# A one-layer hybrid decoder on eight cores: channel-major inputs, three column blocks, and norm sums moved off TensorE

## The chip, the cores and the metric

The program runs on all 8 cores of one Trainium2 chip, each with one of the eight prompt sequences (2048 positions) and 16 of the 128 samples. Nothing is exchanged between cores; all read the same weights. The metric is the device time of the slowest core in microseconds. Most executions agree within 0.3%; some fall into a second, slower state in which one die's or both dies' granted TensorE clock is lower.

The engines are named as the profile names them: PE is TensorE, PEld its weight loads, DVE the vector engine, ACT the scalar engine, POOL is GpSimd, SP the sync engine that issues most small transfers.

## The reference, cut to what matters

```python
D_MODEL, BATCH, SEQ, DEC_BATCH, DEC_SEQ = 1024, 8, 2048, 128, 1
D_FF, P_DIM, CHUNK, CONV_W = 2816, 256, 128, 3

def layer(h, p, prev_a, prev_ffn, ...):
    xn = rmsnorm(h, g_mix)
    x_a, b_a, c_a, uv, ga, gb = split(xn @ w_in)          # 7168 columns
    a_conv, new_a = causal_dwconv(c_a * x_a, w_conv_a, prev_a)
    y_a = (b_a * a_conv) @ w_out_a
    u, v = split(gelu(uv)); v = rmsnorm(v, g_v)
    s = chunk_spatial(v, w_spatial, b_spatial)            # 128-position chunks
    y_b = (u * s) @ w_out_b
    h = h + (sigmoid(ga) * y_a + sigmoid(gb) * y_b) @ w_o
    up = rmsnorm(h, g_ffn) @ w_up                          # 5632 columns
    up_c, new_ffn = causal_dwconv(up, w_conv_ffn, prev_ffn)
    fa, fb = split(up_c)
    h = h + (gelu(fa) * fb) @ w_down
    gate = sigmoid(rmsnorm(h, g_ple) @ w_ple_gate)
    return h + gate * (p @ w_ple), new_a, v[last chunk], new_ffn
# the same layer for prompt and samples, then a final rmsnorm
```

## The kernel before

It keeps activations with channels on the partitions and positions along the row, and goes over the sequence in two passes of 1024 positions. Stages within a pass, by the letters that the code uses: AB (load, norm, v), C (short convolution), D (spatial gating), E (merge), F (output projection), G (up projection and its convolution), H (down projection), I (gate and final norm), O (y out). Weights stream through a ring of eight slots. Each block has 512 positions; the 16 samples are a third, 16-column block of pass 1.

Four parts matter. First, x arrives with positions on the partitions, and TensorE transposes it in and y out:

```python
for hf in range(2):                                   # x in, per 128 positions
    for kk in range(4):
        P.op("pe", lambda e, ...: e.transpose(out=pz[:, kk*128: kk*128+rows],
             in_=xt[0:rows, k*128:(k+1)*128], identity=idf[0:rows, 0:rows]), ...)
# ... and stage O, per 128 positions: 8 transposes of h, then a scaling, then the store
```

Second, a norm's sum of squares is eight matmuls with a matrix of ones per block, each fed by a square of ACT:

```python
class NormAcc:
    def add(self, k, b):
        while len(self.pend_mm) >= 2:
            self.pend_mm.pop(0)[1]()
        # ...
        def emit_sq():
            sq, sqr = sqR.get()
            P.op("act", ... activation(out=sq[:, 0:n], in_=h[:, k, c0:c0+n], func=AF.Square))
            self.pend_mm.append((bi, lambda: P.op("pe", lambda e: e.matmul(
                pst[:, 0:n], lhsT=ones[:], rhs=sq[:, 0:n], start=(cnt == 0), stop=(cnt == 7)), ...)))
```

Third, in stage G the up-projected rows are copied to SBUF with a two-column carry ahead of them, and the taps of the convolution read that copy:

```python
P.op("act", ... copy(out=ux[:, 2+q*512: 2+(q+1)*512], in_=pp[:, 0:512]))
P.op("act", ... activation(out=acc[:, q*512:(q+1)*512], in_=pp, func=AF.Identity, scale=wcf(2, cc)))
for tap in (0, 1):
    P.op("dve", ... scalar_tensor_tensor(out=acc[:, 0:1024], in0=ux[:, tap:tap+1024],
         scalar=wcf(tap, cc), in1=acc[:, 0:1024], op0=ALU.mult, op1=ALU.add))
# ... one channel pair later: gelu on ACT, product act = gelu(a) * b on POOL (1024 wide)
```

Fourth, a weight slab is a slice of the plain matrix, rows of 256 columns, and the first slab is asked for only when all of x has landed:

```python
src = w[:, c0:c0 + 256].rearrange("(k p) n -> p k n", p=128)
xtra = [("xst", 0), ("xst", 1), ("xst", 2), ("xst", 3), ("pst",)] if i == 0 else []
P.dma("pool", (lambda e, ...: e.dma_start(out=dst, in_=src)), f"wr{s}", reads=xtra, writes=res)
```

Of the kernel before, what the change touches and what calls it, by code (L numbers as in the profile page):

```python
# [19 lines left out]
TT = 1040  # L20

class Prog:
# [11 lines left out]
    def _deps(self, eng, reads, writes):  # L34
        deps = {}
        for r in reads:
            t = self.last_write.get(r)
            if t is not None and deps.get(t[0], 0) < t[1]:
                deps[t[0]] = t[1]
        for w in writes:  # L40
            t = self.last_write.get(w)
            if t is not None and deps.get(t[0], 0) < t[1]:
                deps[t[0]] = t[1]
            rd = self.readers.get(w)
            if rd:
                for k, v in rd.items():
                    if deps.get(k, 0) < v:
                        deps[k] = v
# [96 lines left out]

def bcast_mid(ap, reps):
    pairs = [list(x) for x in ap.ap]
    assert len(pairs) == 2, pairs
    return bass.AP(ap.tensor, ap.offset, [pairs[0], [0, reps], pairs[1]])

def build_program():
# [9 lines left out]
    x_d = din("x", [SEQ, D]); xs_d = din("xs", [NS, D])  # L161
    p_d = din("p", [SEQ, PD]); ps_d = din("ps", [NS, PD])
    sa_d = din("sa", [NS, 2, D]); sf_d = din("sf", [NS, 2, 2 * DFF])
    g_mix = din("g_mix", [D]); g_v = din("g_v", [D]); g_ffn = din("g_ffn", [D])
    g_ple = din("g_ple", [D]); g_final = din("g_final", [D])
    w_in = din("w_in", [D, NIN]); w_conv_a = din("w_conv_a", [3, D])
    w_out_a = din("w_out_a", [D, D]); w_out_b = din("w_out_b", [D, D]); w_o = din("w_o", [D, D])
    w_spatial = din("w_spatial", [8, 128, 128]); b_spatial = din("b_spatial", [8, 128])
    w_up = din("w_up", [D, 2 * DFF]); w_conv_ffn = din("w_conv_ffn", [3, 2 * DFF])
    w_down = din("w_down", [DFF, D]); w_ple_gate = din("w_ple_gate", [D, D]); w_ple = din("w_ple", [PD, D])  # L170
    ident_d = din("ident", [128, 128]); tril_d = din("tril", [128, 128])

    y_d = dout("y", [SEQ, D]); ys_d = dout("ys", [NS, D])
    ca_d = dout("ca", [2, D]); cas_d = dout("cas", [NS, 2, D])
    cv_d = dout("cv", [128, D]); cvs_d = dout("cvs", [NS, D])
    cf_d = dout("cf", [2, 2 * DFF]); cfs_d = dout("cfs", [NS, 2, 2 * DFF])

    es = contextlib.ExitStack()
    with es:
        def sb(name, shape, dt):  # L180
# [3 lines left out]
        xn = sb("xn", [128, 8, TT], BF16)  # L184
        R1 = sb("R1", [128, 9216 + 2 * 8 * TT], BF16)
        vn3 = R1[:, 0:9216].rearrange("p (t f) -> p t f", t=9)
        m3 = R1[:, 0:8 * TT].rearrange("p (k t) -> p k t", k=8)
        ab = R1[:, 9216:9216 + 8 * TT].rearrange("p (k t) -> p k t", k=8)
        us = R1[:, 9216 + 8 * TT:9216 + 16 * TT].rearrange("p (k t) -> p k t", k=8)
        act = R1[:, 0:22 * TT].rearrange("p (k t) -> p k t", k=22)  # L190
        R1f = R1[:, :].bitcast(F32)
        xst = R1f[:, 0:8192].rearrange("p (t f) -> p t f", t=8)
        pst_all = R1f[:, 8192:10240].rearrange("p (t f) -> p t f", t=8)
        xss = R1f[0:NS, 10240:11264]
        pss_all = R1f[0:NS, 11264:11520]
        pT = sb("pT", [128, 2, TT], BF16)
        ring = sb("ring", [128, 8, 2048], BF16)
        rs = sb("rs", [128, TT], F32)
        idf = sb("idf", [128, 128], F32); idb = sb("idb", [128, 128], BF16)
        tril = sb("tril", [128, 128], F32)  # L200
        ones = sb("ones", [128, 128], BF16)
        WsT = sb("WsT", [128, 8, 128], BF16)
        Ds = sb("Ds", [16, 8, 16], BF16)
        w00 = sb("w00", [16, 8], F32)
        bbcw = sb("bbcw", [128, 1032], F32)
        bbc = bbcw[:, 0:1024].rearrange("p (j t) -> p j t", j=8)
        gvbc = sb("gvbc", [128, 1024], F32)
        gfbc = sb("gfbc", [128, 1024], F32)
        rtok = sb("rtok", [128, 16], F32)
        cols1 = sb("cols1", [128, 64], F32)  # L210
        cols2 = sb("cols2", [128, 128], F32)
        wcfT = sb("wcfT", [128, 132], F32)
        carry_a = sb("carry_a", [128, 2, 8], F32)
        carry_f = sb("carry_f", [128, 2, 44], F32)
        saT = sb("saT", [128, NS, 2, 8], F32)
        sfT = sb("sfT", [128, NS, 2, 44], F32)
        oAs = sb("oAs", [128, NS, 2, 8], F32)
        oFs = sb("oFs", [128, NS, 2, 44], F32)
        ssv = sb("ssv", [128, 16], F32)
        rv = sb("rv", [128, 16], F32)  # L220
        big = [sb(f"big{i}", [128, 1024], F32) for i in range(4)]
        pbf = [sb(f"pbf{i}", [128, 256], BF16) for i in range(2)]
        sqall = sb("sqall", [128, 2064], BF16)
        sqb = [sqall[:, i * 512:(i + 1) * 512] for i in range(4)]
        sqwide = sqall[:, :].bitcast(F32)
        NTMP = 8
        tmpall = sb("tmpall", [128, NTMP * 516], F32)
        tmpf = [tmpall[:, i * 516:(i + 1) * 516] for i in range(NTMP)]
        widef = [tmpall[:, 2 * j * 516: 2 * j * 516 + 1032] for j in range(NTMP // 2)]
        ps = [es.enter_context(nc.psum_tensor(f"pq{i}", [128, 512], F32)) for i in range(8)]  # L230

        bigR = Rot([(big[i], ("big", i)) for i in range(4)])
        pinR = Rot([(None, pbf[i], ("pin", i), ("pbf", i)) for i in range(2)])
        sqR = Rot([(sqb[i], ("sq", i)) for i in range(4)])
        tmpR = Rot([(tmpf[i], [("tmp", i, "a"), ("tmp", i, "b")]) for i in range(NTMP)])
        wideR = Rot([(widef[j], [("tmp", 2 * j, "a"), ("tmp", 2 * j, "b"), ("tmp", 2 * j + 1, "a"), ("tmp", 2 * j + 1, "b")])
                     for j in range(NTMP // 2)] + [(bbcw, ["bbc"]), (sqwide, [("sq", i) for i in range(4)])])
        class PsRot:
            def __init__(self):
                self.i = 0  # L240
                self.reserved = set()

            def get(self):
                while True:
                    b = self.i % 8
                    self.i += 1
                    if b not in self.reserved:
                        return ps[b], ("ps", b)

            def reserve(self):  # L250
                t, r = self.get()
                self.reserved.add(r[1])
                return t, r

            def release(self, r):
                self.reserved.discard(r[1])

        psR = PsRot()
        scr = sb("scr", [128, 2], F32)
        epsT = sb("epsT", [128, 1], F32)  # L260

        def pstag(i):
            return ("ps", i)

        def gcol(gi, k):
            return cols1[:, gi * 8 + k: gi * 8 + k + 1]

        def wca(tap, j):
            return cols1[:, 32 + tap * 8 + j: 32 + tap * 8 + j + 1]

        def wcf(tap, c):
            r = tap * 44 + c
            if r < 128:
                return cols2[:, r:r + 1]
            return cols1[:, 56 + r - 128: 56 + r - 128 + 1]

        def stage_inputs(pss):
            r0 = pss * 1024
            P.dma("sp", (lambda e: e.dma_start(out=pst_all, in_=p_d[r0:r0 + 1024, :].rearrange("(t q) f -> q t f", q=128))),
                  "xp", reads=["R1busy"], writes=[("pst",)])  # L280
            for hf in range(4):
                P.dma("sp", (lambda e, hf=hf: e.dma_start(
                    out=xst[:, hf * 2:(hf + 1) * 2, :],
                    in_=x_d[r0 + hf * 256: r0 + (hf + 1) * 256, :].rearrange("(t q) f -> q t f", q=128))),
                    f"xs{hf}", reads=["R1busy"], writes=[("xst", hf)])
            if pss == 1:
                P.dma("sp", (lambda e: e.dma_start(out=xss, in_=xs_d[:, :])), "xq0", reads=["R1busy"], writes=[("xss",)])
                P.dma("sp", (lambda e: e.dma_start(out=pss_all, in_=ps_d[:, :])), "xq1", reads=["R1busy"], writes=[("pss",)])

        outs_tok = []  # L290
        stg0, stg0r = big[0], ("big", 0)
        stg1, stg1r = big[1], ("big", 1)
        setup = []

        def sdma(eng, out, in_, writes, **kw):
            setup.append((eng, out, in_, writes, kw))

        sdma("sp", idf[:], ident_d[:, :], ["idf"])
        sdma("sp", tril[:], tril_d[:, :], ["tril"])
        sdma("sp", bbcw[:, 0:1024], b_spatial.rearrange("j t -> (j t)").partition_broadcast(128), ["bbc"])  # L300
        sdma("sp", gvbc[:], g_v.partition_broadcast(128), ["gvbc"])
        sdma("sp", gfbc[:], g_final.partition_broadcast(128), ["gfbc"])
        sdma("sp", stg0[0:8, 0:128], g_mix.rearrange("(j p) -> j p", p=128), [stg0r])
        sdma("sp", stg0[8:16, 0:128], g_ffn.rearrange("(j p) -> j p", p=128), [stg0r])
# [85 lines left out]
        def slab_items():  # L390
            items = []

            def std(w, c0):
                items.append(("std", w, c0))
# [796 lines left out]
```

## Time and profile before

| | before |
|---|---|
| median of 6 runs | 1310.89 us (1308.83 to 1511.96; two slow) |
| spans of the cores in the profile | 1296.3 to 1311.1 us |
| mean granted clock of the cores | 0.963 to 0.968 |
| PE busy | 94% |

The chain and the windows are in the prediction.

### The profile page before, as it was taken

What the parts mean: (1) busy time and instruction counts of PE and PEld (TensorE: products, weight loads), DVE (VectorE), ACT (ScalarE), POOL (GpSimd) and SP (SyncE); (2) the same over time, 40 slices, a digit from 0 to 9 for tenths busy, and PEclk for the clock granted to TensorE, in tenths of its full rate; (3) what the DMA queues carried; (4) which work ended last, traced back from release to release, by engine and by line L of the source; (5) the groups of instructions that cost most, each with busy time, mean ns of one, the idle gap of its engine ahead of it and who ended that gap; (6) DMA issues with size and microseconds to landing.
All of it is one profiled execution on the core that took longest, in us unless ns stands there. A gap on an engine that the chain in (4) does not pass through costs nothing.

```text
span 1311.1 us, 21098 instructions; the slowest of 8 cores (1296.3 to 1311.1 us)
## 1 busy us (share of the span) xinstructions
PE 1228.5 (94%) x7121; PEld 619.6 (47%) x7121; DVE 727.7 (56%) x877; ACT 565.7 (43%) x1089; POOL 382.6 (29%) x399
## 2 busy tenths in 40 slices
PE   4599999999899999999579999999999999999897
PEld 3374454444344444434457445544444444444445
DVE  2417672112699996136540766422247999971376
ACT  3462222112488884125376222211137787831254
POOL 1011111322167776110101121123213666641000
PEclk9699999999899999999779999999998999999998
DMA  7954762577545646976913475344445665289403
GB/s 231 133 71 65 96 86 28 69 95 94 65 65 65 91 51 98 107 99 169 195 14 49 66 104 77 53 65 64 65 65 75 80 73 65 27 93 100 57 24 131
DMA packets 196392, 108.94 MB, mean 83 GB/s; under 512 B 48475, under 2 KB 190607, under 8 KB 196287
## 3 DMA queue, kind: packets, MB, share of 16 engines
q0 software_dynamic: 183136, 81.80, 51.3%
q1 hardware_dynamic: 13151, 25.79, 6.2%
q8 instruction: 60, 0.98, 0.3%
q14 instruction: 45, 0.37, 0.1%
HBM read 179.42 MB, written 9.95 MB: 144 GB/s over the span
## 4 chain that ended last, share of the span: by engine, by line
PE 87%; DMA 5%; DVE 3%; ACT 2%; issue 2%; SPq 1%; POOL 0%; DVEq 0%; ACTq 0%; POOLq 0%
PE pq L549 66%; PE pq L1000 12%; PE pq L663 5%; DMA s_ring<-w_in 2%; PE pq L508 2%; DMA s_R<-x 1%; DMA y<-s_big 1%; DVE s_xn L541 1%; ACT s_sqall L505 1%; PE pq L1075 1%; DVE s_big L1131 1%; PE pq L632 1%; PE pq L818 1%; PE pq L1108 1%; ACT s_rs L531 0%
## 5 line engine op out<-in xcount | busy, mean ns | idle before, releaser
L549 PE MATMUL pq<-s_xn,s_ring 128*128 128x512 bf16 (+1 forms) x4000 | 740.5, 340 | 1.9 <-ACT s_rs L531 0.9
L549 PEld LDWEIGHTS pq<-s_xn,s_ring 128*128 128x128 bf16 x4000 | 335.4, 98 | 380.3 <-issue 15.7
L549 PE MATMUL pq<-s_R,s_ring 128*128 128x512 bf16 (+1 forms) x960 | 181.7, 337 | 0.0
L929 DVE SCALAR_TENSOR_TENSOR s_big<-s_tmpall,s_cols,s_big 128x1024 f32<-128x1024 f32 x92 | 156.4, 1725 | 13.5 <-ACT s_tmpall L917 7.6
L1000 PE MATMUL pq<-s_R,s_ring 128*128 128x512 bf16 (+1 forms) x880 | 160.9, 337 | 0.0
L505 ACT ACTIVATE s_sqall<-s_h 128x512 bf16<-128x512 f32 (+1 forms) x160 | 82.7, 541 | 173.8 <-DVE s_h L1006 117.6
L549 PEld LDWEIGHTS pq<-s_R,s_ring 128*128 128x128 bf16 x960 | 81.1, 97 | 90.7
L451 POOL DMA_DIRECT2D s_ring<-w_in x56 | 49.4, 893 | 232.4 <-PE pq L663 128.4
L1000 PEld LDWEIGHTS pq<-s_R,s_ring 128*128 128x128 bf16 x880 | 73.5, 97 | 82.7
L862 DVE SCALAR_TENSOR_TENSOR s_tmpall<-s_tmpall,pq 128x512 f32<-128x512 f32 (+1 forms) x40 | 23.4, 584 | 145.9 <-PE pq L549 145.7
L938 POOL TENSOR_TENSOR s_R<-s_big 128x1024 bf16<-128x1024 f32 x30 | 83.6, 2785 | 27.5 <-ACT s_tmpall L917 13.4
L921 ACT COPY s_tmpall<-pq 128x512 f32<-128x512 f32 x120 | 70.4, 587 | 48.4 <-PE pq L549 43.4
L868 POOL TENSOR_TENSOR s_R<-s_tmpall 128x512 bf16<-128x512 f32 (+1 forms) x40 | 41.9, 1056 | 166.0 <-DVE s_tmpall L865 126.5
L1006 DVE TENSOR_TENSOR s_h<-pq,s_h 128x512 f32<-128x512 f32 (+1 forms) x40 | 22.8, 586 | 111.7 <-PE pq L1000 102.9
L858 ACT ACTIVATE s_tmpall<-pq 128x512 f32<-128x512 f32 (+1 forms) x40 | 20.6, 514 | 148.5 <-PE pq L549 148.5
L923 ACT ACTIVATE s_big<-pq,s_cols 128x512 f32<-128x512 f32 x120 | 83.7, 697 | 0.0
L541 DVE SCALAR_TENSOR_TENSOR s_xn<-s_h,s_cols,s_rs 128x512 bf16<-128x512 f32 (+1 forms) x120 | 68.2, 643 | 20.7 <-ACT s_rs L534 16.2
L663 PE MATMUL pq<-s_ring,s_xn 128*128 128x256 bf16 (+1 forms) x544 | 67.8, 292 | 10.7 <-DMA s_ring<-w_in 10.6
L508 PE MATMUL pq<-s_sqall,s_ones 128*128 128x512 bf16 (+1 forms) x160 | 53.9, 354 | 24.8 <-ACT s_sqall L505 21.1
L663 PEld LDWEIGHTS pq<-s_ring,s_xn 128*128 128x128 bf16 (+1 forms) x544 | 55.9, 103 | 22.6 <-issue 12.6
L746 ACT ACTIVATE s_tmpall<-s_tmpall,s_cols 128x512 f32<-128x512 f32 x32 | 23.1, 722 | 91.5 <-DVE s_tmpall L742 91.5
L926 POOL COPY s_carry_f<-s_tmpall 128x2 f32<-128x2 f32 x60 | 44.7, 750 | 60.3 <-ACT s_tmpall L921 60.2
(139 smaller groups left out, 1147.3 us busy)
## 6 DMA issues: line engine op xcount, KB each, us to landing
s_ring<-w_in POOLq DMA_DIRECT2D x56, 512.0 KB, 8.7
s_ring<-w_up POOLq DMA_DIRECT2D x44, 512.0 KB, 7.6
s_ring<-w_down POOLq DMA_DIRECT2D x16, 704.0 KB, 8.9
s_R<-x SPq DMA_DIRECT2D x8, 1024.0 KB, 19.1
y<-s_big SPq DMA_DIRECT2D x16, 512.0 KB, 5.2
s_ring<-w_out_a POOLq DMA_DIRECT2D x8, 512.0 KB, 9.6
s_ring<-w_out_b POOLq DMA_DIRECT2D x8, 512.0 KB, 11.3
s_ring<-w_o POOLq DMA_DIRECT2D x8, 512.0 KB, 9.2
```

The lines of the kernel that those rows point to most:

```text
L451: P.dma("pool", (lambda e, dst=dst, src=src: e.dma_start(out=dst, in_=src)), f"wr{s}", reads=xtra, writes=res)
L505: P.op("act", lambda e: e.activation(out=sq[:, 0:n], in_=h[:, k, c0:c0 + n], func=AF.Square), reads=[("h", k, bi)], writes=[sqr])
L508: "pe", lambda e: e.matmul(pst[:, 0:n], lhsT=ones[:], rhs=sq[:, 0:n], start=(cnt == 0), stop=(cnt == 7)),
L541: P.op("dve", lambda e, k=k: e.scalar_tensor_tensor(out=xn[:, k, c0:c0 + n], in0=h[:, k, c0:c0 + n], scalar=gcol(gi, k), in1=rs[:, c0:c0 + n],
L549: P.op("pe", lambda e, k=k: e.matmul(pt[:, 0:n], lhsT=wv[:, k, u * 128:(u + 1) * 128], rhs=src[:, k, c0:c0 + n], start=(k == 0), stop=(k = ...
L663: P.op("pe", lambda e, k=k, q2=q2, wv=wv, pz=pz, c0=c0, rows=rows: e.matmul(pz[0:rows, q2 * 256:(q2 + 1) * 256], lhsT=xn[:, k, c0:c0 + row ...
L921: P.op("act", lambda e, ux=ux, pp=pp, q=q: e.copy(out=ux[:, 2 + q * 512: 2 + (q + 1) * 512], in_=pp[:, 0:512]), reads=[ppr], writes=uxr)
L923: P.op("act", lambda e, acc=acc, pp=pp, cc=cc, q=q: e.activation(out=acc[:, q * 512:(q + 1) * 512], in_=pp[:, 0:512], func=AF.Identity, sc ...
L926: P.op("pool", lambda e, ux=ux, cc=cc: e.tensor_copy(out=carry_f[:, :, cc], in_=ux[:, NP2:NP2 + 2]), reads=uxr, writes=[("carry_f", cc)])
L929: P.op("dve", lambda e, acc=acc, ux=ux, cc=cc, tap=tap: e.scalar_tensor_tensor(out=acc[:, 0:NP2], in0=ux[:, tap:tap + NP2], scalar=wcf(tap ...
L938: P.op("pool", lambda e: e.tensor_tensor(out=act[:, c, 0:NP2], in0=aa[:, 0:NP2], in1=ab_[:, 0:NP2], op=ALU.mult), reads=aar + abr_, writes ...
L1000: P.op("pe", lambda e, c=c: e.matmul(pD[:, 0:n], lhsT=wd[:, c, :], rhs=act[:, c, c0:c0 + n], start=(c == 0), stop=(c == 21)), reads=wdr + ...
```

## The change

The intent is to take from TensorE all that is not a weight tile, and to fill the seam between the passes.

- The host lays x, p, y and the states out with channels first and packs each weight slab contiguously. All transposes go; the 196392 DMA packets of the profile before become 46731.
- Blocks of 384, 384 and 256 positions; the 16 samples are 16 more columns of the third block of pass 0.
- The two columns of history a convolution needs are computed again (386 columns for 384) rather than carried.
- Norm sums: ACT squares, POOL adds them up; two ones matmuls per block are left. The first block keeps eight.
- The taps of stage G read PSUM directly.
- Fourteen matmuls of the ones tile, whose result nothing reads, run (L518).
- x of pass 1 is loaded, squared and normed during stage H of pass 0; y of pass 0 is scaled and stored during stage C of pass 1.

The diff cut to its core (`...` marks cuts):

```diff
-    x_d = din("x", [SEQ, D]); xs_d = din("xs", [NS, D])
+    xt_d = [din("xt0", [128, 8, TT]), din("xt1", [128, 8, 1024])]
...
-                    src = w[:, c0:c0 + 256].rearrange("(k p) n -> p k n", p=128)
+                dst = ring[:, s:s + ns, :].rearrange("p a b -> p (a b)")[:, 0:nel]   # slab contiguous in DRAM
...
+            return [dict(idx=0, c0=0, n=384, s=0), dict(idx=1, c0=384, n=384, s=0),
+                    dict(idx=2, c0=768, n=256, s=(NS if p == 0 else 0))]
...
+        class Norm:
...
+                P.op("act", ... activation(out=out, in_=src, func=AF.Square))
+                if 0 < q < 7:
+                    P.op(self.eng, ... tensor_tensor(out=dst, in0=acc, in1=out, op=ALU.add))
...
+                    group(pt[:, 0:N], [(ones[:], ssb[:, s, 0:N], ...), (ones[:], sqb[:, s, 0:N], ...)], ["ones"], ptr)
...
-                            P.op("act", lambda e, ...: e.copy(out=ux[:, 2 + q * 512: 2 + (q + 1) * 512], in_=pp[:, 0:512]),
-                                out=acc[:, 0:NP2], in0=ux[:, tap:tap + NP2], scalar=wcf(tap, cc), in1=acc[:, 0:NP2], ...
+                                out=acc[:, c0:c0 + n], in0=pt[:, tap:tap + n], scalar=wcf(tap, cc), in1=acc[:, c0:c0 + n], ...
...
+                        for _ in range(2):              # stage C of pass 1: y of pass 0, two pieces per block
+                            if yq and not vq:
+                                yq.pop(0)()
...
+                anrm = Norm(1, "pool", early=True, src=lambda k, b: xst[(k, b["idx"])])   # stage H of pass 0
...
-            STAGE_MARKS.append(("O", pss, len(P.ops["pe"])))    # y transposes, scaling, stores
+                fn.to_y(b0, 3, 2); fn.to_y(b1, 3, 2); fn.to_y(b2, 3, 4)
```

## The prediction

> **What bounds the kernel now**
>
> I read the page first: the busy shares, the forty slices and the chain that ended last.
>
> ```profile
> span 1311.1 us, 21098 instructions; the slowest of 8 cores (1296.3 to 1311.1 us)
> PE 1228.5 (94%) x7121; PEld 619.6 (47%) x7121; DVE 727.7 (56%) x877; ACT 565.7 (43%) x1089; POOL 382.6 (29%) x399
> ...
> PE   4599999999899999999579999999999999999897
> ...
> PEclk9699999999899999999779999999998999999998
> ...
> PE 87%; DMA 5%; DVE 3%; ACT 2%; issue 2%; SPq 1%; POOL 0%; DVEq 0%; ACTq 0%; POOLq 0%
> ```
>
> TensorE carries 87% of the chain. It is thin in three places only: the first slice or two, the seam between the two passes over the sequence (slices 19 and 20), and the end. Outside those a change pays only if it removes TensorE work; inside them it pays by removing waits.
>
> Next the chain in order of time (start, duration, what), for what one matmul costs and how the start goes.
>
> ```profile
> 8.30 19.29 DMA s_R<-x
> 28.27 2.75 POOL s_ring L451 x3
> 31.02 24.82 DMA s_ring<-w_in
> ...
> 200.61 117.41 PE pq L549 x544
> ...
> 520.98 4.75 PE pq L1000 x22
> 525.94 4.75 PE pq L1000 x22
> ```
>
> 117.41 us / 544 is 215.8 ns for a 512-column matmul, with no gap in 117 us: a dense stretch is at the rate of the array. The down projection shows 4.96 us from group to group with 4.75 us of its own work: the missing 0.21 us is one "ones" matmul of the norm. In the same view eight 16-column matmuls (the samples, pass 1) take 0.18 to 0.20 us, some 24 ns each, and four 128-column ones 0.22 us. The start is a line of two transfers: x lands, and only then the weights are asked for; TensorE runs steadily from 56 us.
>
> Then busy time by stretch (columns: stretch, length, PE, PEld, DVE, ACT, POOL busy, granted clock, DMA share, GB/s).
>
> ```profile
> 346.00:501.00 155.00, 154.58 (x704) 69.58 (x705) 144.63 (x90) 123.63 (x241) 105.19 (x79) 0.98 0.52 63
> 501.00:581.00 80.00, 79.55 (x368) 35.81 (x366) 21.80 (x23) 15.10 (x24) 20.62 (x17) 1.00 0.76 97
> 581.00:616.00 35.00, 32.32 (x132) 13.36 (x133) 25.81 (x39) 17.12 (x30) 1.63 (x2) 0.90 0.87 203
> 616.00:649.00 33.00, 18.78 (x119) 12.24 (x116) 18.75 (x29) 13.51 (x20) 4.50 (x6) 0.84 0.74 137
> 649.00:680.00 31.00, 22.29 (x123) 15.27 (x124) 16.07 (x31) 23.09 (x51) 0.00 (x0) 0.72 0.37 76
> ```
>
> 616 to 680 is the seam: 64 us in which y is transposed back and stored and the next x transposed and normed, at a clock of 0.84 and 0.72. 346 to 501 is the up projection: DVE at 144.6 of 155 us is almost as full as PE, so the new form of that stage must be priced on DVE too.
>
> **What the Trainium skill says**
>
> "TensorE: Matmul & The Clock Gate", section "Back-to-back issue gap": N/2.4 + 2.5 ns warm. The trace agrees: 215.8 ns at 512 columns, 55 at 128. I use it to interpolate: 162.5 ns at 384 columns, 115.8 at 272, 109.2 at 256.
>
> Same page, "What's actually happening": the clock falls to half after an idle window of about 3.4 us and comes back after as long a busy one. The trace agrees in kind: the granted clock is 1.00 in dense stretches and 0.72 to 0.84 in the seam. So removing a wait also removes a slow restart.
>
> "VectorE: DVE Perf Modes", section on the TRN2 errata: fp32 two-input operations take (N+151)/0.96 ns. The trace agrees: 686 to 692 ns at 512 columns against 691. Hence 557 ns at 384 and 424 at 256.
>
> "SBUF — State Buffer", section "Who interferes with whom": a DVE instruction with two SBUF inputs and a GpSimd instruction that reads SBUF exclude each other for the whole instruction; with at most one SBUF input DVE does not contend. The first half shows in the taps of the up projection, both inputs in SBUF (minimum/median/maximum ns):
>
> ```profile
> L929 DVE SCALAR_TENSOR_TENSOR s_big<-s_tmpall,s_cols,s_big x92: 1271/1283/3452, 355.8 to 1155.6; 128x1024 f32<-128x1024 f32 x92
> L862 DVE SCALAR_TENSOR_TENSOR s_tmpall<-s_tmpall,pq x40: 164/686/690, 205.9 to 951.7; 128x512 f32<-128x512 f32 x32, 128x16 f32<-128x16 f32 x8
> ```
>
> The second half is only consistent with the 690 ns maximum of the PSUM-fed row; no busy GpSimd tests it there.
>
> **The change part by part**
>
> It is a rewrite around the same matmuls. There are 1248 weight tiles per pass; 64 of them (v) are used as moving operand, leaving 1184.
>
> TensorE work of before, full clock: 2 x 1184 x 215.8 = 511 + 511; v, 544 x 109.2 = 59; samples, 1184 x 24 ns = 28; ones matmuls, 128 x 216 = 28; spatial 7; fp32 transposes of x and y, some 270 at 0.11 (full clock) to 0.2 us (half clock), about 45. Sum 1190 us. The other 121 us are waits and half clock.
>
> What happens to each:
> - The host lays x, p and y out channels first, so the transposes go: -45 us.
> - The samples stop being 16-column matmuls and become 16 more columns of the third block of pass 0: 1184 x 16/2.4 = 8 us instead of 28: -20.
> - The sum of squares is added up on GpSimd (on DVE at the start), so a norm needs two ones matmuls per block instead of eight; the first block keeps eight. About 8 us remain of 28: -20.
> - Blocks of 384, 384, 256 in place of 512, 512: one more fixed 2.5 ns per tile and pass, 2368 x 2.5: +6.
> - The convolutions' carry becomes two recomputed columns: 480 tiles x 6 blocks x 2/2.4 ns: +2.
> TensorE after: 1190 - 45 - 20 - 20 + 6 + 2, about 1113 us. A sum stage by stage (564 + 550) gives 1114.
>
> The waits:
> - Start. At some 250 GB/s of HBM reads (p and x, 5 MB, land between 7 and 27.6 us), x of block 0 with the weight slab issued beside it is in at about 14 us, normed at 21; slabs 0 to 3 are in at about 33, and the v stage, 31 us of work, ends at about 59 instead of 85. Loss 26 us, before 52.
> - Seam. Pass 1's x is loaded and normed under pass 0's down projection; pass 0's y is scaled and stored under pass 1's conv stage. 24 more DVE operations of 557 ns, 13 us, fit there: DVE per block in that stage is 4 x 0.57 = 2.3 us, PE 24 x 162.5 ns = 3.9 us. Loss about 0.
> - Up projection. A tap reads PSUM directly: per channel pair DVE does 4 x (557 + 557 + 424) = 6.15 us, PE 16 x (163 + 163 + 110) = 7.0. PE stays the bound, by 12%.
> - Stage borders and the contention of the new GpSimd adds with DVE in the output and gate stages (6 adds of about 1 us a block): 15 us in all.
> - End. After the last matmul: tanh, two DVE operations, the Ln table load, Ln, Exp, then 24 scalings for all three blocks (16 x 557 + 8 x 424 = 12.3 us) and 4 MB of stores behind them. About 22 us, as before (1290 to 1311).
>
> Sum: 1114 + 26 + 0 + 15 + 22 = 1177 us. I say 1178.
>
> **The rivals**
>
> 1. DVE takes over in the up projection. For: 6.15 against 7.0 us is thin, and GpSimd still multiplies 1024-wide tiles beside it (2.35 us at best). If the lock hits PSUM-fed taps too, a pair costs 8.5 us and 44 pairs lose 1.5 us each: +66, about 1240. Against: the page on SBUF, and one SBUF input each.
> 2. Denser TensorE work brings the clock down. For: two of six runs of before took 1478 and 1512 us. Against: 117 us without a gap ran at 1.00 on this core, and every core averaged at least 0.963. At 13/16 throughout the dense work would be 1371 us and the time about 1434. I give it two or three chances in a hundred for the fast runs.
> 3. The start stays bound by transfers: 8 MB are wanted in 33 us on all cores. At 180 GB/s instead of 250 the v stage ends 12 us later: 1190.
> 4. DVE backs up in the gate stage (two operations, an added norm, GpSimd's lock): 5 to 10 us a pass, 1190 to 1200.
> 5. The seam and start were hidden anyway. The windows speak against it: PE is busy 41 of 64 us there, on transposes that go too.
>
> **Range and chances**
>
> Unknown are the start (+-8), the borders and contention (-8 to +25), the end (+-6) and rival 1. 1150 to 1215 us should hold it 8 times in 10. Within 2% of before means above 1285 us, which needs rival 2 or two other rivals in full: faster 0.96, same 0.03, slower 0.01.
>
> **What would show it**
>
> Right: TensorE steady from about 25 to 60 us on; no thin slice in the middle; no transposes; ones matmuls down to some 60; one 384-column matmul at 162.5 ns; DVE taps at 557 with a maximum near the median; granted clock 0.98 or more outside the first slice and the end. Wrong: taps of 800 ns and more, gaps in PE in the up projection released by DVE, dense stretches under 1.00, or a seam that is still there because the early norm or a weight slab came late.

## More of the kernel before

One more view is used later: who TensorE waited for (columns: total us, times, longest us).

```profile
PE pq L508 <- ACT s_sqall L505: 21.1, 18, 2.2
PE pq L622 <- DVE s_pbf L606: 14.9, 4, 8.0
PE pq L663 <- DMA s_ring<-w_in: 10.6, 4, 4.7
```

The largest is the ones matmul (L508) waiting for the square that feeds it: 18 waits, so the norms cost waits beside their matmuls. The other two belong to the start and the seam between the passes.

## The result, and the profile after

| | before | after |
|---|---|---|
| median, same chip | 1308.94 us (1305.38 to 1542.66, 16 runs) | 1205.31 us (1204.21 to 1206.63, 8 runs) |
| spans of the cores | 1296.3 to 1311.1 us | 1197.7 to 1203.5 us |
| mean granted clock | 0.963 to 0.968 | 0.986 to 0.988 |

The ratio is 0.9212, 95% interval 0.9201 to 0.9223. A ratio here is the mean time of one kernel's fast runs over that of the other's fast runs of the same rounds, so it is not quite the ratio of the medians quoted. The changed kernel is faster by 7.9%.

The page of the changed kernel, in the lines that answer those of before:

```profile
span 1203.5 us, 24319 instructions; the slowest of 8 cores (1197.7 to 1203.5 us)
PE 1137.8 (95%) x7852; PEld 756.7 (63%) x7852; DVE 701.8 (58%) x1354; ACT 482.1 (40%) x1019; POOL 360.6 (30%) x411
...
PE   5998999999999999999998999999998999999992
...
PEclk9999999999999999999998999999999999999996
...
PE 76%; DVE 8%; DMA 6%; ACT 4%; issue 3%; POOL 2%; DVEq 0%; SPq 0%; ACTq 0%; POOLq 0%
```

Slice 1 (counted from 0), 5 before, is 9; slices 19 and 20, which were 5 and 7, are 9, with an 8 behind them. PE has 7852 instructions instead of 7121 and is busy 91 us less. But the chain of waits has only 76% of TensorE where before had 87%: it now leads through a load of 37 us (below) and more often through DVE and ACT. TensorE itself does not wait more: all rows of the view of its waits add up to 48 us, 73 before.

The chain of waits at the start (start, duration, what). The first weight slab is now asked for at 1.65 us, beside x; the next three, which the second line shows, as soon as the first block of x is there.

```profile
3.01 10.96 DMA s_h<-xt
...
14.52 7.87 DMA s_ring<-win
```

x of block 0 lands at 14.0 us, where all of x was in at 27.6 us before.

Who TensorE waits for now:

```profile
PE pq L356 <- POOL s_ssb L419: 12.6, 7, 3.5
PE pq L406 <- ACT s_wide L405: 9.2, 4, 5.8
PE pq L356 <- ACT s_sqb L416: 8.2, 2, 5.8
PE pq L356 <- DVE s_xn L446: 5.0, 12, 2.3
PE pq L356 <- DVE s_R L611: 4.1, 4, 1.5
```

L356 is the helper that issues all projections and the two ones matmuls of a norm. The first row is POOL's running sum arriving late, the third the eighth square, the fifth the output of the short convolution. Some 6 us of the first and third rows fall after the last projection, in the tail, and 9.2 us of the second before the first.

Where the time is, by stretch of the changed kernel (columns as in the prediction's table):

```profile
341.00:487.00 146.00, 145.87 (x991) 95.72 (x992) 132.49 (x252) 86.18 (x190) 56.69 (x38) 1.00 0.49 75
...
638.00:660.00 22.00, 16.23 (x96) 9.97 (x96) 7.92 (x16) 9.72 (x19) 0.55 (x2) 0.84 0.53 89
660.00:734.00 74.00, 71.99 (x496) 47.22 (x495) 54.82 (x107) 17.96 (x38) 5.90 (x15) 1.00 0.73 143
```

The up projection (first row) has no gap on PE. The seam (second row) still has one: 5.8 us without work, at a mean clock of 0.84.

To see what each stage lost, I took its limits from TensorE's timeline and set them against its tiles (columns/2.4 + 2.5 ns each, two or more ones matmuls added):

| stage | from, to (us) | length | work | lost |
|---|---|---|---|---|
| start and v, pass 0 | 0, 59.4 | 59.4 | | (predicted end 59) |
| C, pass 0 | 59.4, 149.3 | 89.9 | 85.0 | 4.9 |
| D | 149.3, 182.8 | 33.5 | 32.0 | 1.5 |
| E, F, G | 182.8, 486.1 | 303.3 | 298.0 | 5.3 |
| H | 486.1, 570.2 | 84.1 | 79.1 | 5.0 |
| I | 570.2, 609.2 | 39.0 | 35.5 | 3.5 |
| v, pass 1 | 609.2, 637.1 | 27.9 | 28.0 | 0 |
| C, pass 1 | 637.1, 732.5 | 95.4 | 84.6 | 10.8 |
| D | 732.5, 765.9 | 33.4 | 31.3 | 2.1 |
| E, F, G | 765.9, 1065.0 | 299.1 | 293.6 | 5.5 |
| H | 1065.0, 1142.1 | 77.1 | 77.1 | 0 |
| I | 1142.1, 1180.6 | 38.5 | 35.0 | 3.5 |
| tail | 1180.6, 1203.5 | 22.9 | | (predicted 22) |

The lost column adds up to 42 us. The prediction gave 15 to stage borders and contention and 0 to the seam. The difference, 27 us, is the whole difference between 1178 and 1205. The experiments go after it.

Two of the causes can be read. In pass 0's stage C the chain of waits shows one transfer:

```profile
65.07 37.08 DMA s_R<-gv
...
102.24 1.28 DVE s_wide L582
```

That is the gain of the v norm, 512 KB, needed by DVE to write the samples' v out (L582); the convolution's operations stand behind it in DVE's queue and waited too. The load was issued after two stores of the carried state, one of them 352 KB in runs of 64 bytes, which took 36.6 us.

In the seam, TensorE's timeline (start, length, what, in brackets the idle time ahead and what ended it):

```profile
637.78 0.28 PE L356 MATMUL pq<-s_ssb,s_ones 128*128 128x272 bf16 x1
643.83 0.38 PE L356 MATMUL pq<-s_sqb,s_ones 128*128 128x272 bf16 x1 [5.77 <-ACT s_sqb L416]
```

The final norm of pass 0 delays every square by one step. The last square of the last block is therefore emitted only when the norm is asked for, in pass 1, behind all squares of the v stage in ACT's queue. 0.38 for 272 columns, against 0.28 in the line above, shows the half clock that follows the gap.

### The profile page after: what moved, and what is told of

Read it like the earlier page. It is cut to its first block, busy times and chain, and to the rows that moved or that the text cites. A ratio compares the mean times of both kernels' runs of the same rounds, so it can differ in the third digit from the quotient of the medians.

```text
span 1203.5 us, 24319 instructions; the slowest of 8 cores (1197.7 to 1203.5 us)
## 1 busy us (share of the span) xinstructions
PE 1137.8 (95%) x7852; PEld 756.7 (63%) x7852; DVE 701.8 (58%) x1354; ACT 482.1 (40%) x1019; POOL 360.6 (30%) x411
## 4 chain that ended last, share of the span: by engine, by line
PE 76%; DVE 8%; DMA 6%; ACT 4%; issue 3%; POOL 2%; DVEq 0%; SPq 0%; ACTq 0%; POOLq 0%
PE pq L356 64%; PE pq L875 11%; DMA s_R<-gv 3%; DVE s_xn L446 3%; DMA s_h<-xt 2%; POOL s_ss L419 1%; ACT s_wide L562 1%; DVE s_wide L960 1%; DVE s_h L478 1%; DVE s_h L962 1%; DMA s_ring<-win 1%; ACT s_R L555 1%; PE pq L626 1%; DVE s_h L461 0%; ACT L436 0%
## 5 line engine op out<-in xcount | busy, mean ns | idle before, releaser
L356 PE MATMUL pq<-s_xn,s_ring 128*128 128x386 bf16 (+5 forms) x5184 | 789.9, 309 | 9.2 <-DVE s_R L611 4.1
L356 PEld LDWEIGHTS pq<-s_xn,s_ring 128*128 128x128 bf16 x5184 | 499.0, 97 | 270.2 <-issue 21.1
L814 DVE SCALAR_TENSOR_TENSOR s_wide<-pq,s_cst,s_wide 128x384 f32<-128x384 f32 (+1 forms) x528 | 278.5, 568 | 30.6 <-ACT s_wide L806 2.3
L806 ACT ACTIVATE s_wide<-pq,s_cst 128x384 f32<-128x384 f32 (+1 forms) x264 | 137.5, 548 | 131.5 <-DVE s_wide L814 114.6
L875 PE MATMUL pq<-s_R,s_ring 128*128 128x384 bf16 (+2 forms) x1056 | 156.8, 311 | 0.0
L821 POOL TENSOR_TENSOR s_R<-s_wide 128x1024 bf16<-128x1024 f32 x44 | 103.8, 2360 | 173.1 <-DVE s_wide L814 154.3
L655 DVE SCALAR_TENSOR_TENSOR s_wide<-s_wide,pq 128x384 f32<-128x384 f32 (+2 forms) x96 | 49.2, 513 | 172.6 <-PE pq L356 172.6
L419 POOL TENSOR_TENSOR s_ss<-s_ss,s_sq 128x384 f32<-128x384 f32 (+2 forms) x105 | 99.4, 950 | 134.4 <-ACT s_sq L416 126.9
L356 PE MATMUL pq<-s_R,s_ring 128*128 128x384 bf16 (+2 forms) x768 | 119.8, 309 | 0.0
L416 ACT ACTIVATE s_sq<-s_h 128x384 f32<-128x384 f32 (+2 forms) x120 | 57.7, 488 | 136.2 <-DVE s_h L881 72.7
L356 PEld LDWEIGHTS pq<-s_R,s_ring 128*128 128x128 bf16 x768 | 75.0, 98 | 37.0
L446 DVE SCALAR_TENSOR_TENSOR s_xn<-s_h,s_cst,s_rsb 128x384 bf16<-128x384 f32 (+2 forms) x120 | 62.3, 591 | 35.2 <-ACT s_rsb L437 35.2
L881 DVE TENSOR_TENSOR s_h<-pq,s_h 128x384 f32<-128x384 f32 (+2 forms) x48 | 23.5, 512 | 95.2 <-PE pq L875 95.2
L356 PE MATMUL pq<-s_ring,s_xn 128*128 128x256 bf16 (+1 forms) x544 | 65.8, 279 | 6.0 <-DVE s_xn L446 4.4
L356 PEld LDWEIGHTS pq<-s_ring,s_xn 128*128 128x128 bf16 (+1 forms) x544 | 53.5, 99 | 18.5 <-issue 11.1
```

The lines of the kernel that those rows point to most:

```text
L356: P.op("pe", lambda e, l=l, r=r, q=q: e.matmul(out, lhsT=l, rhs=r, start=(q == 0), stop=(q == n - 1)), reads=list(reads) + list(rd), write ...
L416: P.op("act", lambda e: e.activation(out=out, in_=src, func=AF.Square), reads=rd, writes=[w])
L419: P.op(self.eng, lambda e: e.tensor_tensor(out=dst, in0=acc, in1=out, op=ALU.add), reads=[sr, w], writes=[dw])
L446: P.op("dve", lambda e, src=src, dst=dst, k=k: e.scalar_tensor_tensor(out=dst, in0=src, scalar=gcol(gi, k), in1=r[:, 0:N], op0=ALU.mult, o ...
L655: P.op("dve", lambda e, tt=tt, py=py: e.scalar_tensor_tensor(out=tt[:, 0:N], in0=tt[:, 0:N], scalar=1.0, in1=py[:, 0:N], op0=ALU.add, op1= ...
L806: P.op("act", lambda e, acc=acc, pt=pt, cc=cc, c0=c0, n=n: e.activation(out=acc[:, c0:c0 + n], in_=pt[:, 2:2 + n], func=AF.Copy, scale=wcf ...
```

## The experiments

All ran beside the kernel before on the same chip, in three sessions on three chips (its medians 1309.0, 1308.9 and 1308.5 us). The changed kernel had 1205.31 us before them, and 1203.61 in the third session as a control:

> The changed kernel once more, unedited, as a control on this chip: 1203 to 1207 us, ratio to the kernel before 0.920 to 0.923.

Measured: 1203.61 us (1202.7 to 1254.39, 5 runs), ratio 0.9198 (0.9179 to 0.9218). So a difference under about 2 us is not to be read as one, and differences of 2 to 5 us are checked below by the length of the stage that was edited: a median over the eight cores of the profiled execution, from the first and last matmuls of the stage.

### 1. The gain load ahead of the state stores

```diff
                 v_of(2, 1)
+                load(gvx[:, :], gv_d.partition_broadcast(128), "gvb", gvxr)
                 setup_small()
                 setup_state()                  # the state stores
...
-            load(gvx[:, :], gv_d.partition_broadcast(128), "gvb", gvxr)
+            if p == 1:
+                load(gvx[:, :], gv_d.partition_broadcast(128), "gvb", gvxr)
```

> The changed kernel with one transfer moved: in pass 0 the broadcast load of the v gain is issued before the two scattered state stores instead of behind them. Theory (the load only waits because it is queued behind stores of 64-byte runs): DVE's 6.2 us wait for it at about 102 us goes, with it the 3.4 us of PE idle and the half-clock window after it, so 5 to 6 us less than the changed kernel's 1205 us, about 1199 to 1200 us. Rival (the broadcast load is slow in itself, or held up by the weight loads): it still lands late, DVE waits as before, 1204 to 1206 us.

Measured: 1200.25 us (1199.25 to 1312.06), ratio 0.9171 (0.9148 to 0.9194): 5.1 us less than the first measurement of the changed kernel, 3.4 less than the control. Stage C of pass 0 takes 84.9 us, with 85.0 us of work, in this and the three other kernels with the edit, and 85.8 to 89.3 us in the nine executions without it. The transfers of this kernel's gain, in duration of the issue (minimum, median, maximum ns):

```profile
L261 SPq DMA_DIRECT2D s_R<-gv x2: 341/469/597, 30.1 to 566.7; - x2
```

The same row had a maximum of 22123 ns in the changed kernel: even the instruction that issues the load was held there for 22 us. It now lands 17.0 us after its issue at most, and nothing waits for it. It is also issued 35 us earlier (30.1 instead of 65.1 us), so that even a slow load would have been in time; what speaks for the theory is that the issue and the transfer themselves became short.

### 2. The delayed square flushed at the end of the gate stage

```diff
                 nextn[0] = fn
+                for bb in blocks:
+                    fn.flush(bb["idx"])
```

> The changed kernel with the last delayed square of pass 0's final norm issued at the end of the gate stage instead of after pass 1's v stage. Theory (TensorE sits 5.8 us at the start of pass 1's conv stage because that square stands behind the v stage's squares and the table load in ACT's queue, and then restarts at half clock): 5.8 us of wait and 3.4 us of half clock go, 9 us less, about 1196 us. Rival (the conv stage of pass 1 is set by DVE, which carries pass 0's y scaling too, so the wait is made good behind it): DVE backlog takes its place, at most 3 us less, 1202 to 1205 us.

Measured: 1200.97 us (1199.0 to 1202.44), ratio 0.9177 (0.9153 to 0.92): 4.3 us less (2.6 against the control), between the two expectations. Stage C of pass 1 falls from 95.2 to 90.7 us. The 5.8 us wait is gone from TensorE's timeline, but the waits for the convolution's output rose from 4.1 us in 4 to 6.6 us in 9: stage C of pass 1 has a second limit close behind the first.

### 3. The y scaling in the merge stage

```diff
-                        for _ in range(2):                 # in stage C of pass 1
-                            if yq and not vq:
-                                yq.pop(0)()
...
                         stage_merge(p, ip * 2 + u, u, b, ...)
+                        for _ in range(2):
+                            if yq:
+                                yq.pop(0)()
```

> The changed kernel with pass 0's y scaling, its stores and the reload of h moved from pass 1's conv stage to pass 1's merge stage, where DVE is busy a quarter of the time. Theory (the conv stage of pass 1 is DVE-bound by it: DVE stands in order behind an ACT round trip in each block, so its free time cannot be used): the 3.4 us of PE waits there and the late start of the spatial stage go, 4 to 6 us less, 1199 to 1201 us. Rival (it is not DVE that sets that stage, or the stores and loads meet the weight loads of the merge stage and the output stage waits for h): 1205 us or more.

Measured: 1201.28 us (1199.01 to 1244.7), ratio 0.9177 (0.9152 to 0.9201): 4.0 us less (2.3 against the control). Stage C of pass 1 falls from 95.2 to 92.4 us and stage D behind it from 33.5 to 31.5. Waits for the convolution's output fell from 4.1 to 0.4 us. The edit moved the stores of y and the reload of h too, but in the changed kernel no scaling in stage C (L461) had idle time ahead of it: DVE did not stand there for a transfer. The second limit of stage C was DVE: in 660 to 734 us it is busy 54.8 of 74 us, yet the chain convolution (DVE to ACT to DVE) leaves it standing between its links, and two scalings of 0.6 us per block on top were too many. In the merge and output stages (766 to 895 us) DVE is busy 33 of 129 us.

### 4. The three together

> The three edits of the first batch together: the early gain load, the early last square, pass 0's y scaling moved to pass 1's merge stage. One by one they took 5.1, 4.3 and 4.0 us off 1205.3. Theory (the early square alone could not give its 9 us because the DVE-bound conv stage behind it took half back; with the y scaling gone it gives them in full): 4 to 5 for the load, 9 for the square, 4 to 5 for the scaling, 17 to 19 us, so 1186 to 1188 us, and the conv stage of pass 1 at 84 to 86 us. Rival (each edit is worth what it was alone, the square has only 4 us in it): 13 us, 1192 us.

Measured: 1188.99 us (1187.23 to 1323.55), ratio 0.9084 (0.9066 to 0.9102): 16.3 us less, where the three alone add up to 13.4 (14.6 and 8.3 against the control). With an interval of some 3 us on each, the totals alone do not show that the three help each other. The stage does: C of pass 1 takes 84.4 us, 10.8 less than in the changed kernel, where experiments 2 and 3 alone take off 4.5 and 2.8. The seam, two rows for the same stretches as above:

```profile
638.00:660.00 22.00, 22.00 (x152) 14.61 (x151) 13.17 (x26) 7.66 (x18) 0.37 (x2) 1.00 0.33 58
660.00:734.00 74.00, 74.00 (x535) 50.33 (x533) 52.31 (x101) 23.30 (x50) 7.99 (x19) 1.00 0.61 99
```

TensorE is busy all of the 96 us, at full clock. The seam and the C stages were worth more than half of the 27 us.

### 5. Norm sums of the down projection on DVE

```diff
-            nrm = Norm(p, "pool")
+            nrm = Norm(p, "dve")
...
-                anrm = Norm(1, "pool", early=True, ...)
+                anrm = Norm(1, "dve", early=True, ...)
```

> The changed kernel with the sums of squares in the down projection (its own norm, and the early norm of pass 1's x) added on DVE, not on GpSimd: DVE is busy a third of that stage, an add of 384 columns takes 0.56 us there against 1.0 us plus 0.2 us of hand-over on GpSimd. Theory (the down projection of pass 0 loses 2.6 us of PE waits and a half-clock window of 3.4 us to the chain of GpSimd adds): both go, 4 to 6 us less, 1199 to 1201 us. Rival (the chain only shows the wait; the down projection waits for the scaling on DVE or for x, or DVE's adds come in the way of the residual adds): 1204 to 1208 us.

Measured: 1207.48 us (1205.34 to 1229.63), ratio 0.9219 (0.9198 to 0.924): no gain. The wait only changed its name. TensorE's waits in this kernel:

```profile
PE pq L356 <- DVE s_ssb L419: 2.6, 1, 2.6
```

A POOL add of 384 columns takes 1.03 us, one on DVE 0.56. But the adds of the block that is waited for now stood behind eight normalisations of the block before in DVE's queue (548.3 to 552.6 us), so the run shows that this move does not help, not that the speed of the adds has no part in the wait. Experiment 9 tests the other candidate, when the sum is asked for.

### 6. Eight ones matmuls again

Blocks of stages F (both passes) and H (pass 1) sum their squares on TensorE, as before the change.

```diff
             nrm = Norm(p, "pool")
+            nrm.pe = 2                                   # squares on ACT, then one ones matmul each
...
+                    self.late.append((bi, lambda: P.op("pe", lambda e: e.matmul(pt[:, 0:N], lhsT=ones[:], rhs=out,
+                                      start=(q == 0), stop=(q == 7)), ...)))
+                    while len(self.late) > 2:
+                        self.late.pop(0)[1]()
```

> One part of the change undone: in the output stage of both passes and in the down projection of pass 1 the squares are summed over channels by eight ones matmuls per block again, not added up on GpSimd with two ones matmuls. TensorE gets 3 norms x 6 x (162 + 162 + 112 ns), 7.9 us more work. Theory (the border losses between output and up projection are the chain of six GpSimd adds of 1.2 us each that a norm's ones matmul waits for): 6.5 us of waits go at the same time, so the time is within +-3 us of the changed kernel, 1202 to 1208 us, with no wait for GpSimd left at those borders. Rival (the border waits are the scaling on DVE that follows, so they stay): 7 to 9 us more, 1212 to 1214 us.

Measured: 1230.23 us (1229.36 to 1312.18), ratio 0.9399 (0.9376 to 0.9421): 25 us more, above both expectations. TensorE's waits in this kernel:

```profile
PE pq L412 <- ACT s_sq L411: 20.0, 14, 3.5
```

The time lies where the edit is: E to G are 8.6 and 9.2 us longer, H of pass 1 6.2. 54 more matmuls are 54 x 0.145 = 8 us of work (the mean of two of 162.5 and one of 109.2 ns); 20.0 us are waits of the ones matmul for its square, against 6 us less of waiting for POOL. The remaining 3 us are not separated; the clock is 0.981 to 0.984 instead of 0.986 to 0.988. It is the kind of wait whose row of 21.1 us led the kernel before. So moving the sums off TensorE was worth far more than its matmuls, in this form: as before the change, a ones matmul is held back by two squares and a PSUM bank is kept for the sum (the cut leaves that out). A longer delay was not tested.

### 7. Taps from an SBUF copy

The same blocks and columns, but ACT copies the up-projected rows to SBUF and the taps read the copy.

```diff
+                        P.op("act", ... copy(out=ux[:, 0:n + 2], in_=pt[:, 0:n + 2]))
-                                out=acc[...], in0=pt[:, tap:tap + n], scalar=wcf(tap, cc), in1=acc[...]
+                                out=acc[...], in0=ux[:, tap:tap + n], scalar=wcf(tap, cc), in1=acc[...]
```

> One part of the change undone: in the up projection ACT copies the bank to SBUF and the two taps read that copy, so a tap has two SBUF inputs as before the change; block sizes and all else stay. ACT gets 2.7 us more per channel pair, 7.4 in place of 4.7 us, which alone makes the stage ACT-bound (7.4 against 7.05 us for PE). Theory (with two SBUF inputs a tap shuts out the GpSimd product and is shut out by it, 2.4 us per pair): DVE needs 6.8 + 2.4 = 9.2 us a pair, the stage takes some 200 us instead of 144 in each pass, about 1310 us, taps with a maximum of 2.5 us or more. Rival (no such exclusion for 384-column taps; only ACT binds): about 1230 to 1245 us, taps at 0.61 us with a maximum near it.

Measured: 1284.35 us (1282.79 to 1366.9), ratio 0.9814 (0.9792 to 0.9837): 79 us more, nearer the theory. The taps of the changed kernel (minimum, median, maximum ns), from PSUM:

```profile
L814 DVE SCALAR_TENSOR_TENSOR s_wide<-pq,s_cst,s_wide x528: 474/607/620, 332.6 to 1070.3; 128x384 f32<-128x384 f32 x132, 128x256 f32<-128x256 f32 x44
```

and of this kernel, from SBUF:

```profile
L816 DVE SCALAR_TENSOR_TENSOR s_wide<-s_sq,s_cst,s_wide x528: 473/614/2742, 335.8 to 1157.9; 128x384 f32<-128x384 f32 x132, 128x256 f32<-128x256 f32 x44
```

The medians are the same, the maximum is 2742 instead of 620: most taps run at the same speed. 42 of the 528 take over 1 us, and every one of these begins or stands during a POOL product (2.5 us); the first in the stage's steady part begins at 369.6 us, 0.6 us into a product, and ends at 371.8, 0.3 us after it. In the changed kernel 44 such products run beside the taps and none of these is slow. DVE is busy 360 instead of 285 us with the taps. From one product to the next it takes 9.07 us in the middle of the stage, where it took 6.95. DVE's row of twelve taps takes some 8.8 of the 9.07 us, while ACT, with the copies, is busy 95 of 140 us: DVE sets the stage, and the 54 us that TensorE waits for ACT's copies come from behind it. The 75 us of DVE time are nearly all of the 79; E to G are 35 and 38 us longer.

### 8. The final scaling of block 0 earlier

In pass 1 the first block's y is scaled and stored inside the gate stage, during the third block, not after it.

```diff
+                    if p == 1 and 8 * bi + i == 17:
+                        fn.to_y(b0, 3, 2)
...
-                fn.to_y(b0, 3, 2)
                 fn.to_y(b1, 3, 2)
```

> The changed kernel with the final scaling of block 0 in pass 1 issued while the gate stage of block 2 still runs, not after it. Theory (the end is 12 us of scaling on DVE in a row after the last matmul, and DVE has some 7 us free in the gate stage): 2 to 4 us less, 1201 to 1203 us. Rival (DVE is as full as PE in the gate stage, so the scaling only pushes the last blocks' own DVE work back): within 1 us of the changed kernel, 1204 to 1207 us.

Measured: 1206.03 us (1204.18 to 1207.78), ratio 0.9219 (0.9199 to 0.924): no gain. TensorE's waits for the gate product on DVE rose from 3.4 us:

```profile
PE pq L356 <- DVE s_wide L960: 6.2, 6, 2.5
```

In the gate stage DVE is busy 34.4 of 41 us; what leaves the tail delays the stage ahead of it. The gate stage of pass 1 and the tail together take 62.9 us here and 60.7 in the changed kernel.

### 9. The next norm asked for one unit later

```diff
-                if p == 0 and b["idx"] == 0:
+                if p == 0 and b["idx"] == 1:
                     anrm.to_xn(nb[2], 0)
```

> The changed kernel with one move: in the last down-projection units of pass 0 the sums for the norm of the next x's first block are turned into a normalised block one unit later. Theory (placement: a sum is asked for only some 7 us after it was started): the 2.0 us wait of TensorE for GpSimd's sum and the 3.4 us of half clock behind it go, about 1200 us, 4 to 5 below the changed kernel. Rival (the sum is late by more than one unit hides, or the wait moves to the next user of the normalised block): 1204 to 1207 us.

Measured: 1205.62 us (1203.14 to 1206.25, 4 runs), ratio 0.9211 (0.919 to 0.9232), beside the control's 0.9198: no gain. Stretches of this kernel:

```profile
545.00:565.00 20.00, 20.00 (x138) 13.31 (x137) 13.45 (x21) 7.81 (x19) 10.02 (x13) 1.00 0.40 68
565.00:609.00 44.00, 40.22 (x269) 25.30 (x267) 37.38 (x72) 25.84 (x55) 19.62 (x22) 1.00 0.36 61
609.00:638.00 29.00, 26.35 (x240) 23.17 (x237) 1.10 (x3) 19.79 (x36) 7.05 (x12) 1.00 0.92 138
```

The wait of stage H is gone: 20.00 of 20 us busy, where the changed kernel has 17.44. Stage H of pass 0 takes 79.9 us in this and the two later kernels with the edit, 82.2 in the control and 83.9 in the changed kernel. But stage I behind it takes 41.6 us in all three, and 39.1 in both of the others: what was won is lost there. In the profile the scalings of the last block of the next x (L446, to 564.9 us) now run just ahead of the gate stage's own eight, and TensorE's first eight matmuls wait 0.2 us each for one of these. So the placement was the cause of that wait, and removing it moved the loss to the next stage. The rival's second half was right. (The 26.35 of 29 us in the third row is no new loss: the seam's wait for the delayed square begins here already at 635.1 us, within the stretch.)

### 10. All repairs, and a later load of the second block

Experiment 1, 2, 3 and 9 in one kernel:

> The three repairs together (early gain load, the delayed square flushed, the y scaling in the merge stage) plus the later normalisation. Theory (the later normalisation adds its own 4 to 5 us to the 1189 of the three): about 1184 us. Rival (nothing left to gain there): 1188 to 1190 us.

Measured: 1187.89 us (1187.46 to 1188.46, 5 runs), ratio 0.908 (0.9062 to 0.9099). The later norm adds nothing to the three repairs (1188.99 us, ratio 0.9084), as experiment 9 says. This kernel and that of experiment 4 beat both of the original ones, by 9.2% and by about 1.4% (1.3% against the control).

Then, on top, the second block of x is asked for only when the first has landed:

```diff
         load_h(0, blocks_of(0)[0], 4)
-        load_h(0, blocks_of(0)[1], 4)
+        load_h(0, blocks_of(0)[1], 4, [("h", 7, 0)])
```

> The kernel of the four repairs, and at the very start the load of x's second block is held until the first has landed. Theory (the two loads share the queues' rate, so the first lands about 10 instead of 14 us): 2 to 4 us below the four repairs. Rival (the second block then comes late and TensorE waits there instead): equal to it or up to 3 us above.

Measured: 1193.33 us (1192.43 to 1224.78, 5 runs), ratio 0.9118 (0.9099 to 0.9138): 5.4 us worse. The chain of waits at the start of this kernel:

```profile
2.99 11.28 DMA s_h<-xt
...
14.83 11.13 DMA s_ring<-win
```

The first block lands after 11.28 us; with both in flight it was 11.67 us. So the two loads do not share a rate that binds the first, and the theory falls. Held back, the second block now runs beside the weight slab, which takes 11.13 instead of 8.06 us, and all behind it is later: TensorE is busy 29.4 of the 37 us from 22 to 59 us instead of 34.4. In both kernels the first weight slab, issued at 1.65 us, is in flight beside the first block, and no run holds it back. What bounds the first block's load is left open.

## Why the prediction was right or wrong

The time, 1205 us, is inside the range of 1150 to 1215 and 27 us above the 1178 said. By its own steps:

- **TensorE work**, 1190 down to 1113 us: right. Every stage without a wait has the length of its tiles: v of pass 1 27.9 against 28.0 us, H of pass 1 77.1 against 77.1. Experiment 6 shows that the term for the ones matmuls missed the larger part of their cost: 8 us of work stood beside 20 us of waiting. The prediction counted those waits only within the 121 us of "waits and half clock" of before and did not ask which of them go.
- **Start**: right. The v stage ended at 59.4 us (59 said), block 0 was in at 14.0 us (14 said).
- **Seam, "Loss about 0"**: this step failed. It counted DVE's operations of stage C (2.3 us per block against 3.9 of TensorE) and found room for the 13 us of scalings. It did not count the chain convolution, in which DVE and ACT wait for each other, nor the order of ACT's queue, in which a delayed square stood behind the squares of a whole stage. Measured: 10.8 us lost in stage C of pass 1. Experiments 2, 3 and 4 show both causes, and that the second came out when the first was removed: the stage takes 90.7, 92.4 and 84.4 us in them, with 84.6 us of work.
- **Up projection**: right in its mechanism, with a thinner margin. Taps from PSUM have a maximum of 620 ns beside a median of 607, so they stand for nobody, and TensorE is busy 145.87 of 146 us. A tap was said to take 557 and 424 ns; it took 613 and 479. These are 6.5 us of busy DVE per pair (285 us for 44 pairs, since the records overlap a little) instead of 6.15, against 7.05. Rival 1 did not come; experiment 7 shows what it would have cost: 75 us of DVE time, against the 66 us put down for it.
- **"Stage borders and the contention ... 15 us in all"**: the term that was mis-sized. Measured are 42 us with the seam, so 31 without it. Of that, 4.9 are stage C of pass 0, with a cause that was not in the list at all, a load behind stores (experiment 1). The rest is 26 us: 10.8 in E to G, 5.0 in H, 7.0 in I, 3.6 in D (2.0 of these, in pass 1, went with the y scaling in experiment 3). In E to G some two thirds are read from the timeline: where F borders on G, TensorE stands 1.7 and 1.3 us in pass 0 and 2.3 and 1.2 us in pass 1 for POOL's sums, and 0.2 us each for DVE. A norm's chain of POOL adds takes 1.0 us per link and 0.2 us from one to the next; the prediction counted these adds as load for POOL and not as a chain. In I some 2.0 of the 3.5 us in each pass are read as waits for DVE and ACT, and DVE has no room there (experiment 8); the rest is not read. For H, experiment 5 shows that adds in DVE's queue do not help, and experiment 9 that a later norm does, by 2.3 us or more, which stage I then loses. What would bring both back is open.
- **Tail**: right, 22.9 us (22 said).
- **Rivals 2 to 5**: the granted clock rose, from 0.963 to 0.968 up to 0.986 to 0.988 (rival 2 wrong for the fast runs; its 13/16 was given without a source, and what the record shows of it are slow runs, as one of before at 1536.71 us with 0.80 to 0.81 on four cores). The start was as fast as said (rival 3 wrong). DVE did back up in the gate stage: 3.5 us lost per pass, less than rival 4's 5 to 10. The seam and start were not hidden anyway (rival 5 wrong).

Two of the signs named in advance came out as said only in part: "no thin slice in the middle" holds in tenths, while a 5.8 us gap lies inside one, and the granted clock was under 0.98 outside the first slice and the end in two stretches, 0.91 in 545 to 565 us and 0.84 in 638 to 660 us.

## What to carry to other kernels

When a helper's instruction is moved to a less busy engine, price not only its busy time but the length of the chain that it makes and the moment at which its result is asked for; a queue served in order turns one late entry into a wait for all behind it. Removing a small matmul that waits for another engine in the midst of dense work is worth its wait and not only its work: in experiment 6, 8 us of matmuls came with 20 us of waiting. Take a rewrite that pays off through TensorE's timeline stage by stage against its tiles: the difference shows in which stage to look, and repairs there gave another 1.4%.

## What the Trainium skill lacked or had wrong

- "VectorE: DVE Perf Modes", the section on the TRN2 errata: (N+151)/0.96 ns is given for an fp32 tensor_tensor add. Here it holds for that, L881 with 554 ns at 384 columns against 557, and for two-input operations with a constant as scalar (L774 557 ns). The prediction used it for the taps too, whose scalar comes from a tile. With a per-partition scalar the record is longer: 613 at 384 and 479 at 256 columns against 557 and 424, about 55 ns. The kernel before has it too, 747 against 689 ns at 512 columns. The page has no term for it.

```profile
L814 DVE SCALAR_TENSOR_TENSOR s_wide<-pq,s_cst,s_wide 128x384 f32<-128x384 f32 x352 | 204.7, 613 | 21.4 <-ACT s_wide L806 2.3 <-DVE s_wide L814 0.9
L814 DVE SCALAR_TENSOR_TENSOR s_wide<-pq,s_cst,s_wide 128x256 f32<-128x256 f32 x176 | 80.6, 479 | 9.3
...
L881 DVE TENSOR_TENSOR s_h<-pq,s_h 128x384 f32<-128x384 f32 x32 | 17.2, 554 | 79.9 <-PE pq L875 79.9
```

- "SBUF — State Buffer", section "Who interferes with whom": what it says of one SBUF input beside GpSimd holds, and is shown by experiment 7: at most 620 ns from PSUM, up to 2742 ns from SBUF. How often two such instructions meet depends on the kernel, and no page could give it: here 42 of 528 taps met a product, and the taps' time rose by a quarter.
- "DMA: Bandwidth & Descriptors", section "Specifications", gives 512 bytes as the least size for full rate. The page has no measured rate on this chip for a store in shorter runs: one of 352 KB in runs of 64 bytes took 36.6 us, one of the same size in whole rows 2.8 us, and the load behind the slow one on that queue landed 37.1 us after its issue began, the issue alone taking 22.1.
